# Queries' up-projection in six blocks of 512 columns a layer in place of eight of 384, and the later pairs' attention steps two or four slots later

## The chip, the cores and the metric

The kernel runs on one core of a Trainium2 chip. The metric is the device time of one execution in microseconds. TensorE is called PE in the profile (its weight loads PEld), VectorE DVE, ScalarE ACT, GpSimd POOL, SyncE SP.

## The reference, cut to what matters

Two layers of a streaming encoder at 256 positions, width 2048, all in float32. Each layer reads one input projection and has two branches. What the change touches is the attention branch and, through the order of work, the end of the convolution branch:

```
q  = (rmsnorm(q_down)  @ w_uq ).reshape(.., 16 heads, 192)   # 128 plain + 64 rotary columns a head
kv = (rmsnorm(kv_down) @ w_ukv).reshape(.., 16 heads, 256)   # 128 key + 128 value columns a head
q  = rmsnorm(q, q_norm_g); k = rmsnorm(k ++ k_pe, k_norm_g)  # over a head's 192 columns
q, k = rope on the last 64 columns
o  = chunk-causal softmax attention, then * silu(m_gate), @ w_proj_mla
u  = silu(layernorm(depthwise conv of width 31 (c_a * sigmoid(c_glu)))) * silu(c_gate)
y  = sigmoid(g_conv) * (u @ w_proj_conv) + sigmoid(g_mla) * (o @ w_proj_mla);  x + y @ w_out
```

## The kernel before, in words

**Pieces.** Every product has 256 positions (two halves t = 0, 1 of 128 as stationary operands) and streams weight columns in blocks of at most 512. A block comes in pieces of two 128-row slices of the weights: 8 pieces for a weight of 2048 rows, 2 for one of 512 rows (`wuq`, `wukv`). To keep float32's precision each weight piece is split into a rounded part `hi` (ScalarE: CAST hi<-raw) and the rest `lo` (VectorE: lo<-raw,hi), and so are the activations. A piece is 12 matmuls: 2 slices x 2 halves x 3 terms (high by hi, low by hi, high by lo). Layer 0 has 344 pieces. All instructions pass through a helper, so that every row of the profile says L126, and each engine does its work in the order in which the program issues it.

**How far the engines run ahead.** `product` (L337) issues for piece i first the load, `hi` of piece i + 3 (four `hi` buffers) and `lo` of piece i + 2 (three `lo` buffers), then the 12 matmuls, then `background`. So `lo` of piece i + 2 takes the buffer of piece i - 1.

**Slots.** `background` (L243) ends each piece: one piece is one slot. It runs the steps that `at_slot(n, f)` has put n slots ahead, and then, as far as a budget of VectorE time a slot lets it, the next entries of `fill`, a queue that holds the 31 taps of the convolution of every channel block, then the layernorm over channels (sum, mean by a matmul `mu`, centring, squares, variance by a matmul `var`, factors, `apply` and silu) and `gated`, the product with the turned gate. What `gated` leaves is split into `ycT` (`separated`: hi by ScalarE, lo by VectorE), in four groups c = 0 to 3 of four channel slices, that is of two pieces each.

**The queries' block.** Heads go in pairs b = 0 to 7. The order of a layer has for each pair `uq` (one block of 384 columns: both heads' 192), `ukv` (512 columns), then one long block of 8 pieces (`glu` or `cgate`). `uq_evac` (L685) copies the block out of PSUM on ScalarE and sums the squares; `rotate_q` turns the rotary part on VectorE; the rest of a pair's attention are steps at fixed slots behind `ukv` (STATS_AT 2 to O_AT 34). Products alternate between two pairs of PSUM banks, so a block's evacuation must be over before the next block but one begins.

**The place that forces work.** The convolution's projection (`pconv`, weights `wpc`) begins with piece 281 of layer 0. Ahead of the matmuls of its first block's piece j (p0 to p7 below) stands

```
def before_pconv(j, keep=keep):
    c = j * KS // 4
    while c not in keep["separated"]:
        run_fill()
    pay(keep["separated"][c])
    finish_late()
```

If group c has not been split by then, this issues what is missing at once: after `lo` of piece j + 2, which `product` has issued just before, and ahead of the matmuls of piece j.

Of the kernel before, what the change touches and what calls it, by code (L numbers as in the profile page):

```python
# [19 lines left out]
P = 128  # L20
T = 2
# [66 lines left out]
def order_of_layer():  # L88

    order = [("glu", 0, "win")] + [("down", i, "win") for i in range(len(DOWN_BLOCKS))]  # L90
    order += [("glu", 1, "win"), ("glu", 2, "win")]
    for b in range(NPAIR):
        order += [("uq", b, "wuq"), ("ukv", b, "wukv")]
        if b + 3 < 8:
            order.append(("glu", b + 3, "win"))
        elif b + 1 < NPAIR:
            order.append(("cgate", b - 5, "win"))
    for kind, s in (
        ("cgate", "win"), ("mgate", "win"), ("gmla", "win"), ("pmla", "wpm"),
        ("gconv", "win"), ("pconv", "wpc"), ("wout", "wo"),  # L100
    ):
        order += [(kind, i, s) for i in range(2 if kind == "cgate" else 0, 4)]
    return order


def blocks_of_layer():

    s = {"win": [], "wuq": [], "wukv": [], "wpc": [], "wpm": [], "wo": []}
    for kind, i, stream in order_of_layer():
        s[stream].append(DOWN_BLOCKS[i][1] if kind == "down" else 2 * QK if kind == "uq" else 512)  # L110
    return s


# [1 line left out]
def trunk(ctx: ExitStack, tc: tile.TileContext, xT, x, g_in, pos, win, wuq, wukv, wpc, wpm, wo, cst, rows, invf, out):  # L115
# [108 lines left out]
    def at_slot(ahead, f, vec=0.0, act=0.0, first=False):  # L224
        steps.insert(0 if first else len(steps), (clock[0] + ahead, (vec, act), f))
# [344 lines left out]
    for l in range(DEPTH):  # L570
# [86 lines left out]
        def attention_tiles(A=A, l=l):  # L657
            qk_t = big.tile([P, 16 * SEQ], F32R, tag="big", name=f"qk_t{l}")
            A.nope_t = qk_t[:, : 8 * SEQ].rearrange("p (i h s) -> p i h s", i=4, h=2)
            A.rope_t = qk_t[:, 8 * SEQ : 12 * SEQ].rearrange("p (i h s) -> p i h s", i=2, h=2)  # L660
            A.rope_k = qk_t[:, 10 * SEQ : 14 * SEQ].rearrange("p (i h s) -> p i h s", i=2, h=2)
            A.rope_l = qk_t[:, 12 * SEQ : 14 * SEQ].rearrange("p (h s) -> p h s", h=2)
            gps.memset(A.rope_l.bitcast(F32), 0.0)
            pv = big.tile([P, 4096], F32R, tag="big", name=f"pv{l}")
            A.pt = pv[:, : 2 * 768].rearrange("p (i h q) -> p i h q", i=2, h=2)
            v_parts = [pv[:, 1536 + i * 512 : 2048 + i * 512] for i in range(5)] + [qk_t[:, 14 * SEQ :]]
            v_parts = [a.rearrange("p (t h d) -> p t h d", t=T, h=2) for a in v_parts]
            A.v_split = [v_parts[2 * j : 2 * j + 2] for j in range(3)]
# [3 lines left out]
        def pair_of(b, A=A):
            if b not in A.pairs:


                A.pairs[b] = dict(
                    qk=work2.tile([P, T, 4, 6, 32], F32, tag="qk", name="qk"),
                    qr=work2.tile([P, T, 2, 2, HALF], F32, tag="qr", name="qr"),
                    vh=A.v_split[b % 3][0],
                    vl=A.v_split[b % 3][1],  # L680
                    ss=small.tile([P, 2, T, 2], F32, tag="ss_p", name="ss_p"),
                )
            return A.pairs[b]

        def uq_evac(b, t, ps, pair_of=pair_of):  # L685

            p = pair_of(b)
            act.copy(p["qk"][:, t, :, 0:2, :], ps[:, : 2 * NOPE].rearrange("p (j h c) -> p j h c", j=4, h=2))
            act.copy(p["qr"][:, t].rearrange("p a h c -> p (a h c)"), ps[:, 2 * NOPE :])
            for h in range(2):  # L690
                junk = work.tile([P, 512], F32, tag="junk", name="junk")
                act.activation(
                    junk[:, :QK].rearrange("p (j c) -> p j c", c=32),
                    ps.rearrange("p (j h c) -> p j h c", h=2, c=32)[:, :, h, :],
                    AF.Square, accum_out=p["ss"][:, 0, t, h : h + 1],
                )

        def rotate_q(b, pair_of=pair_of, ccq=ccq, ssq_t=ssq_t):
            p = pair_of(b)
            both = lambda a: a.rearrange("p t (a c) -> p (t a) c", a=2).unsqueeze(2).broadcast_to([P, 2 * T, 2, HALF])  # L700
            qa = work.tile([P, T, 2, 2, HALF], F32, tag="qa", name="qa")
            qb = work.tile([P, T, 2, 2, HALF], F32, tag="qb", name="qb")
            qr = p["qr"].rearrange("p t a h c -> p (t a) h c")
            vec.tensor_mul(qa.rearrange("p t a h c -> p (t a) h c"), qr, both(ccq))
            vec.tensor_mul(qb.rearrange("p t a h c -> p (t a) h c"), qr, both(ssq_t))
            out = p["qk"][:, :, :, 4, :].rearrange("p t (h a) c -> p t h a c", h=2)
            vec.tensor_sub(out[:, :, :, 0, :], qa[:, :, 0], qb[:, :, 1])
            vec.tensor_add(out[:, :, :, 1, :], qb[:, :, 0], qa[:, :, 1])

        def ukv_evac(b, t, ps, pair_of=pair_of):  # L710

            p = pair_of(b)
# [12 lines left out]
        def attention(b, pair_of=pair_of, ss_d=ss_d, kpe=kpe, ccq=ccq, ssq_t=ssq_t, gqk=gqk, A=A):  # L725
            p, st = pair_of(b), {}
            nope_t, rope_t, rope_k, rope_l = A.nope_t, A.rope_t, A.rope_k, A.rope_l
            qk, ss = p["qk"], p["ss"]

            def stats():  # L730

                st["r"] = small.tile([P, 2, T, 2], F32, tag="r_p", name="r_p")
                flat = lambda a: a.rearrange("p a t h -> p (a t h)")
                vec.tensor_add(flat(ss), flat(ss), flat(ss_base))
                rsqrt(flat(st["r"]), flat(ss), gps)
                st["rs"] = st["r"][:, 0]

            def scale_k():
# [20 lines left out]
            def back_in(name):  # L759
                for d, a in st[name]:  # L760
                    fetch(d, a)
# [115 lines left out]
                A.pairs.pop(b)  # L877

            at_slot(STATS_AT, stats, 0.6)
            at_slot(SCALE_AT, scale_k, 0.45, 1.1)  # L880
            at_slot(QK_BACK_AT, lambda: back_in("qk"), first=True)
            at_slot(QK_TURN_AT, blockwise, 1.85)
            at_slot(NOPE_AT, split_nope, 0.0, 1.8)
            at_slot(ROPE_AT, split_rope, 0.0, 2.5)
            at_slot(SCORES_AT, scores, 1.85, 0.35)
            at_slot(EXP_AT, exponentials, 0.0, 3.3)
            at_slot(P_BACK_AT, lambda: back_in("p"))
            at_slot(P_TURN_AT, turn_p, 0.9)
            at_slot(P_SPLIT_AT, split_p, 0.0, 0.8)
            at_slot(VALUES_AT, values)  # L890
            at_slot(O_AT, outputs, 0.62, 0.6)
# [353 lines left out]
        for kind, i, pl in planned:  # L1245
# [22 lines left out]
            elif kind == "uq":  # L1268
                if i == 0:
                    attention_tiles()  # L1270
                product(pl, of_down(0), lambda t, ps, i=i: uq_evac(i, t, ps), costs=(0.0, 2.3))
                at_slot(EVAC_AT + 1, lambda i=i: rotate_q(i), 1.2)
            elif kind == "ukv":
                product(pl, of_down(4), lambda t, ps, i=i: ukv_evac(i, t, ps), costs=(0.0, 2.6))
                attention(i)
                if i == NPAIR - 1:
                    layernorm()
            elif kind == "mgate":
# [64 lines left out]
def _layout(inp):  # L1343
# [7 lines left out]
    for l in range(DEPTH):  # L1351
# [9 lines left out]
    )  # L1361

    pair = lambda n, m: np.arange(2 * n).reshape(2, n)[:, :m].reshape(2, m // 32, 32).transpose(1, 0, 2).reshape(-1)
    val = np.concatenate([h * (NOPE + VH) + NOPE + np.arange(VH) for h in range(2)])
    cols_of = {
        "wuq": np.concatenate([2 * QK * b + pair(QK, QK) for b in range(NPAIR)]),
        "wukv": np.concatenate(
            [2 * (NOPE + VH) * b + np.concatenate([pair(NOPE + VH, NOPE), val]) for b in range(NPAIR)]
        ),
# [36 lines left out]
```

## Time and profile before

| | |
|---|---|
| Time, median of 3 runs | 1877.83 us (1877.79 to 1878.21) |
| The profiled execution | 1877.73 us, of which its span is 1875.9 us |
| PE busy | 1871.8 us (100% of the span) |
| DVE busy | 1577.1 us (84%) |
| ACT busy | 1366.4 us (73%) |
| POOL busy | 486.0 us (26%) |
| mean DMA rate | 237 GB/s |

The time is the span and 1.8 us around it. The span is cut into what each engine did; a row of a timeline gives the start, the time taken, the engine, the operation with the tiles it writes and reads, and how many like it follow. A matmul's row lasts from its issue to its modelled end, longer than the distance to the next matmul, so that the pace of PE is read from starts.

### The profile page before, as it was taken

The page shows a single profiled execution, that of the slowest core. Times are in us where ns is not written, and L with a number is a line of the kernel's source. Part 1 is how long each engine was busy: PE and PEld are TensorE (multiplying, and loading weights), DVE is VectorE, ACT ScalarE, POOL GpSimd, SP SyncE. Part 2 cuts the span into 40 slices and gives each one's busy share as a digit, 9 for nine tenths or more (in the row PEclk, how much of TensorE's full clock was granted, in tenths as well). Part 3 has the DMA queues.
Part 4 walks back from the last instruction along what each step waited for, and adds up shares of the span by engine and source line. Part 5 has one row for each costly group of instructions (what it writes and reads, how often), then busy time and mean ns, then how long its engine had stood idle before and what let it go on. Part 6 is the DMA issues. An engine that isn't in the chain of part 4 may idle for free.

```text
span 1875.9 us, 27403 instructions
## 1 busy us (share of the span) xinstructions
PE 1871.8 (100%) x8673; PEld 1584.2 (84%) x8673; DVE 1577.1 (84%) x2426; ACT 1366.4 (73%) x2468; POOL 486.0 (26%) x942
## 2 busy tenths in 40 slices
PE   9999999999999999999999999999999999999999
PEld 8988888888888888888899888888888888888887
DVE  6898988989999988766679889888899999885664
ACT  7678988888888766544557688888889878474442
POOL 1055555432200000122221555555322000001210
PEclk9999999999999999999999999999999999999999
DMA  9677878777765566678877787887777556667775
GB/s 330 216 258 262 272 242 273 264 241 233 244 204 193 195 208 214 212 237 283 288 231 217 250 272 257 262 279 242 245 237 248 191 196 203 206 209 218 242 249 167
DMA packets 140113, 445.06 MB, mean 237 GB/s; under 512 B 23808, under 2 KB 29440, under 8 KB 139968
## 3 DMA queue, kind: packets, MB, share of 16 engines
q1 hardware_dynamic: 106272, 359.89, 58.9%
q0 software_dynamic: 32832, 82.62, 13.5%
q8 instruction: 68, 1.11, 0.2%
q10 hardware_dynamic: 864, 0.80, 0.1%
q14 instruction: 77, 0.63, 0.1%
HBM read 399.18 MB, written 44.04 MB: 236 GB/s over the span
## 4 chain that ended last, share of the span: by engine, by line
PE 100%; DVE 0%; issue 0%
PE acc L126 97%; PE s L126 2%; PE o_ps L126 1%; PE warm L126 0%; PE acc_end L126 0%; PE var L126 0%; PE mu L126 0%; DVE xres L126 0%
## 5 line engine op out<-in xcount | busy, mean ns | idle before, releaser
L126 ACT CAST hi<-raw 128x1024 fp32r<-128x1024 f32 (+3 forms) x690 | 700.8, 1021 | 408.0 <-PE acc L126 347.4
L126 DVE TENSOR_TENSOR lo<-raw,hi 128x1024 fp32r<-128x1024 f32 (+3 forms) x690 | 814.5, 1182 | 197.2 <-PE acc L126 148.3
L126 PE MATMUL acc<-hi,hT 128*128 128x512 f32 (+2 forms) x1728 | 419.5, 382 | 0.0
L126 PEld LDWEIGHTS acc<-hi,hT 128*128 128x128 f32 x1728 | 319.7, 188 | 59.2
L126 PE MATMUL acc<-hi,h_hi 128*128 128x512 f32 (+2 forms) x864 | 260.9, 383 | 0.0
L126 PE MATMUL acc<-hi,h_lo 128*128 128x512 f32 (+2 forms) x864 | 260.3, 382 | 0.0
L126 ACT ACTIVATE tap<-u_t,cst 128x256 f32<-128x256 f32 x588 | 254.7, 499 | 3.2 <-DVE v_t L126 3.2
L126 PE MATMUL acc<-lo,h_hi 128*128 128x512 f32 (+2 forms) x864 | 229.7, 382 | 0.0
L126 PE MATMUL acc<-lo,hT 128*128 128x512 f32 (+2 forms) x864 | 229.3, 382 | 0.0
L126 DVE TENSOR_TENSOR v_t<-v_t,tap 128x512 f32<-128x512 f32 x294 | 201.9, 687 | 10.1
L126 POOL DMA_DIRECT2D turned<-turn_d x88 | 49.3, 560 | 539.8 <-DVE v_t L126 314.7
L126 PEld LDWEIGHTS acc<-hi,h_lo 128*128 128x128 f32 x864 | 161.3, 188 | 30.2
L126 PEld LDWEIGHTS acc<-lo,h_hi 128*128 128x128 f32 x864 | 160.6, 188 | 30.1
L126 PEld LDWEIGHTS acc<-lo,hT 128*128 128x128 f32 x864 | 160.6, 188 | 29.9
L126 PEld LDWEIGHTS acc<-hi,h_hi 128*128 128x128 f32 x864 | 160.3, 188 | 29.5 <-ACT hi L126 0.4
L126 POOL DMA_DIRECT2D turn_d<-gate x184 | 100.3, 553 | 325.4 <-DVE gate L126 182.6
L126 DVE SCALAR_TENSOR_TENSOR v_t<-u_t,cst,v_t 128x256 f32<-128x256 f32 x372 | 159.5, 479 | 2.3
L126 PE MATMUL acc<-hi,ycT 128*128 128x512 f32 x512 | 127.8, 389 | 0.0
L126 PE MATMUL acc<-hi,oT 128*128 128x512 f32 x512 | 127.8, 389 | 0.0
L126 PE MATMUL acc<-hi,yT 128*128 128x512 f32 x508 | 126.8, 389 | 0.0
L126 PE MATMUL acc<-hi,qkc 128*128 128x512 f32 (+1 forms) x512 | 118.7, 363 | 0.0
L126 PEld LDWEIGHTS acc<-hi,ycT 128*128 128x128 f32 x512 | 96.1, 188 | 20.0
(173 smaller groups left out, 2213.6 us busy)
## 6 DMA issues: line engine op xcount, KB each, us to landing
raw<-in_win SPq DMA_DIRECT2D x382, 512.0 KB, 4.3
raw<-in_wpm SPq DMA_DIRECT2D x64, 512.0 KB, 3.3
raw<-in_wpc SPq DMA_DIRECT2D x64, 512.0 KB, 4.1
raw<-in_wo SPq DMA_DIRECT2D x64, 512.0 KB, 4.7
raw<-in_wukv SPq DMA_DIRECT2D x32, 512.0 KB, 3.7
turned<-turn_d POOLq DMA_DIRECT2D x56, 256.0 KB, 4.8
raw<-in_win SPq DMA_DIRECT2D x32, 384.0 KB, 4.6
raw<-in_wuq SPq DMA_DIRECT2D x32, 384.0 KB, 3.4
```

The source lines that it names most:

```text
L126: ins = getattr(self.engine, name)(*a, **k)
```

## The change

Columns of the queries' weights are laid out anew: per four pairs b, b+1, b+2, b+3 three blocks of 512 hold [plain b, rotary b, rotary b+1], [plain b+1, rotary b+2, rotary b+3] and [plain b+2, plain b+3] (256 plain or 128 rotary columns each). Pairs 3 and 7 have no `uq` block of their own. So a layer has six `uq` blocks of two pieces (12 pieces of 512 columns) in place of eight (16 of 384), and 340 pieces and slots in place of 344.

The plain part of pairs 3 and 7 is parked in the last two heads of `o_sb` and copied on later (`waiting_in`); the rotary squares of pairs other than 0 and 4 are summed apart (`rope_squares`: one ScalarE and one VectorE instruction) and added in `stats`. From pair 3 on all attention steps but `stats` stand 2 slots later behind `ukv` (`d = 2`), for pair 7 4 slots later.

```
     for b in range(NPAIR):
-        order += [("uq", b, "wuq"), ("ukv", b, "wukv")]
+        order += [("uq", 3 * (b // 4) + b % 4, "wuq")] if b % 4 < 3 else []
+        order.append(("ukv", b, "wukv"))
...
+            A.waiting = A.o_sb[:, N_HEADS - 2 :, :].rearrange("p h s -> p (h s)").rearrange("p (t j h c) -> p t j h c", t=T, j=4, h=2)
...
+        def nope_out(b, t, src, A=A, part_of=part_of):
+            if b % 4 == 3:
+                act.copy(A.waiting[:, t].rearrange("p j h c -> p (j h c)"), src)
+            else:
+                act.copy(part_of(b, "qk")[:, t, :, 0:2, :], src.rearrange("p (j h c) -> p j h c", j=4, h=2))
...
+        def rope_squares(b, part_of=part_of):
+            sq = work.tile([P, T, 2, 2, HALF], F32, tag="qa", name="sq")
+            act.activation(sq, part_of(b, "qr"), AF.Square)
+            late.append(lambda: vec.tensor_reduce(part_of(b, "ss")[:, 2], sq.rearrange("p t a h c -> p t h a c"), axis=AX.XY, op=ALU.add))
+
+        def waiting_in(b, A=A, part_of=part_of, squares_of=squares_of):
+            act.copy(part_of(b, "qk")[:, :, :, 0:2, :].rearrange("p t j h c -> p (t j) h c"), A.waiting.rearrange("p t j h c -> p (t j) h c"))
+            for t in range(T):
+                squares_of(b, t, A.waiting[:, t])
+
+        def uq_evac(i, t, ps, nope_out=nope_out, rope_out=rope_out, squares_of=squares_of):
+
+            b = 4 * (i // 3)
+            cols = lambda a: a.rearrange("p (j h c) -> p j h c", h=2, c=32)
+            if i % 3 == 0:
+                nope_out(b, t, ps[:, :256])
+                rope_out(b, t, ps[:, 256:384])
+                rope_out(b + 1, t, ps[:, 384:])
+                squares_of(b, t, cols(ps[:, :384]))
+            elif i % 3 == 1:
+                nope_out(b + 1, t, ps[:, :256])
+                rope_out(b + 2, t, ps[:, 256:384])
+                rope_out(b + 3, t, ps[:, 384:])
+                squares_of(b + 1, t, cols(ps[:, :256]))
+            else:
+                nope_out(b + 2, t, ps[:, :256])
+                nope_out(b + 3, t, ps[:, 256:])
+                squares_of(b + 2, t, cols(ps[:, :256]))
...
+            d = 2 * ((b + 1) // 4)
...
-            at_slot(SCALE_AT, scale_k, 0.45, 1.1)
+            at_slot(SCALE_AT + d, scale_k, 0.45, 1.1)
...
+                d = 2 * (i // 4)
+                if i % 4 < 3:
+                    at_slot(3 + d, lambda i=i: rope_squares(i + 1), 0.4, 0.4)
+                if i % 4 < 2:
+                    at_slot(6 + d, lambda i=i: rotate_q(i + 1), 1.2)
+                elif i % 4 == 2:
+                    at_slot(6 + d, lambda i=i: waiting_in(i + 1), 0.0, 1.6)
+                    at_slot(7 + d, lambda i=i: rotate_q(i + 1), 1.2)
```

**Where it moves instructions, first: the projection of the convolution branch in layer 0.** The matmul of the mean stands behind piece 256 of 344 before and behind piece 255 of 340 now; the projection begins with piece 281 before and 277 now, so 25 pieces lay between them and 22 do now. VectorE's order there before, from `lo` of p2 (lo_8026) to that of p5 (lo_8093); ycT_7834 is the low part, the first `ycT` row is that of c = 2 (for p4 and p5), the second that of c = 3 (for p6 and p7):

```order
L126 TENSOR_TENSOR lo_8026<-raw_7908,hi_8003 128x1024
L126 TENSOR_TENSOR ycT_7834<-v_t,ycT_7833 128x512 x2
L126 TENSOR_TENSOR lo_8050<-raw_7935,hi_8028 128x1024
L126 STREAM_TRANSPOSE turned<-turned 128x512
L126 TENSOR_TENSOR v_t<-turned,v_t 128x2x128 x2
L126 TENSOR_TENSOR lo_8071<-raw_7959,hi_8052 128x1024
L126 TENSOR_TENSOR ycT_7834<-v_t,ycT_7833 128x512 x2
L126 TENSOR_TENSOR lo_8093<-raw_7980,hi_8073 128x1024
```

VectorE's order there now, from `lo` of p6 (lo_8027) over p7 (lo_8051) and the next block's p0 (lo_8072) to its p1 (lo_8097):

```order
L127 TENSOR_TENSOR lo_8027<-raw_7921,hi_8004 128x1024
L127 TENSOR_TENSOR v_t<-turned,v_t 128x2x128 x2
L127 TENSOR_TENSOR ycT_7860<-v_t,ycT_7859 128x512 x2
L127 TENSOR_TENSOR lo_8051<-raw_7947,hi_8029 128x1024
L127 STREAM_TRANSPOSE turned<-turned 128x512
L127 TENSOR_TENSOR v_t<-turned,v_t 128x2x128 x2
L127 TENSOR_TENSOR lo_8072<-raw_7967,hi_8053 128x1024
L127 STREAM_TRANSPOSE turned<-turned 128x512
L127 TENSOR_TENSOR v_t<-turned,v_t 128x2x128 x2
L127 TENSOR_TENSOR ycT_7860<-v_t,ycT_7859 128x512 x2
L127 TENSOR_TENSOR lo_8097<-raw_7985,hi_8074 128x1024
```

The `ycT` of c = 2 stood behind `lo` of p2 and stands behind `lo` of p6; that of c = 3 stood behind `lo` of p4 and stands behind `lo` of p8, the next block's first. In layer 1 the last `ycT` stands ahead of the projection's first `lo` in both kernels. ScalarE has now, from `hi` of p6, first a table load, four silus (v_t), `hi` of p7, the two `ycT` casts of c = 2, `hi` of p8 and p9, and the two casts of c = 3.

**Second: PE at p4 now.** Its order, with what each row waits for (ycT_7859 is the high part, ycT_7860 the low part, acc_0 and acc_1 the banks of the two halves):

```order
L127 MATMUL acc_1_7942<-lo_7963,ycT_7859 128x512 x2
L127 MATMUL acc_0_7941<-hi_7965,ycT_7859 128x512 [waits Activation_49]
L127 MATMUL acc_0_7941<-hi_7965,ycT_7859 128x512
L127 MATMUL acc_0_7941<-hi_7965,ycT_7860 128x512 [waits DVE_49]
L127 MATMUL acc_0_7941<-hi_7965,ycT_7860 128x512
L127 MATMUL acc_1_7942<-hi_7965,ycT_7859 128x512 x2
```

The order of the matmuls is that of before; the first row of p4 (hi_7965) waits for ScalarE's cast of c = 2 and the third for VectorE's low part, which now stand behind `lo` of p6 on their engine. p6 has the same two waits for c = 3.

**Third: ScalarE around the evacuation of the `uq` blocks issued with pairs 5 and 6.** Its order now with pair 5 (su is the evacuation of the `glu` block ahead of `uq`, pr the exponentials of an earlier pair, qk, qr and junk the evacuation of `uq`, first half):

```order
L127 CAST hi_3329<-raw_3188 128x1024
L127 ACT_TABLE_LOAD
L127 ACTIVATE su<-acc_0_3057,rinv_x 128x256
L127 ACTIVATE su<-acc_1_3058,rinv_x 128x256
L127 ACT_TABLE_LOAD
L127 ACTIVATE pr,rinv<-sx,nb,r_p 128x4x32 x2
L127 ACTIVATE pr,rinv<-s_3266,nb,r_p 128x2x4x32 x2
L127 CAST hi_3377<-raw_3216 128x1024
L127 CAST hi_3406<-raw_3251 128x1024
L127 COPY qk<-acc_0_3325 128x4x64
L127 COPY qr<-acc_0_3325 128x128 x2
L127 ACTIVATE junk,ss_p<-acc_0_3325 128x128 x2
```

Before, the exponentials with their table load stood two `hi` casts ahead of the `su` rows with theirs; now both stand in one slot, two `hi` casts ahead of the evacuation of `uq`.

## Rows read from the trace of the kernel before

**Rows 1.** The page: busy time, slices and the chain that ended last, by engine.

```profile
PE 1871.8 (100%) x8673; PEld 1584.2 (84%) x8673; DVE 1577.1 (84%) x2426; ACT 1366.4 (73%) x2468; POOL 486.0 (26%) x942
...
PEclk9999999999999999999999999999999999999999
...
PE 100%; DVE 0%; issue 0%
```

**Rows 2.** Who waited for whom: engine, line, releaser: us, times, longest.

```profile
ACT hi L126 <- PE acc L126: 347.4, 272, 2.6
...
DVE lo L126 <- PE acc L126: 148.3, 115, 2.3
```

**Rows 3.** PE's timeline, first pair: start us, us, instruction, count.

```profile
118.86 1.57 PE L126 MATMUL acc<-hi,qkc 128*128 128x384 f32 x8
...
123.05 2.01 PE L126 MATMUL acc<-hi,qkc 128*128 128x512 f32 x8
...
128.53 0.62 PE L126 MATMUL acc<-hi,h_hi 128*128 128x512 f32 x2
```

**Rows 4.** PE's timeline, convolution's projection, first block, layer 0.

```profile
765.21 1.98 PE L126 MATMUL acc<-hi,ycT 128*128 128x512 f32 x8
...
778.81 1.98 PE L126 MATMUL acc<-hi,ycT 128*128 128x512 f32 x8
```

**Rows 5.** Groups by form, VectorE: count | busy, mean ns of one | idle.

```profile
L126 DVE TENSOR_TENSOR v_t<-turned,v_t 128x256 f32<-128x256 f32 x32 | 11.7, 419 | 0.3
```

**Rows 6.** VectorE's timeline in that projection (idle before and releaser in brackets).

```profile
769.18 1.29 DVE L126 TENSOR_TENSOR ycT<-v_t,ycT 128x512 fp32r<-128x512 f32 x2 [1.49 <-ACT ycT L126]
770.39 1.22 DVE L126 TENSOR_TENSOR lo<-raw,hi 128x1024 fp32r<-128x1024 f32 x1
771.52 0.70 DVE L126 STREAM_TRANSPOSE turned<-turned 128x512 f32<-128x512 f32 x1
772.26 0.76 DVE L126 TENSOR_TENSOR v_t<-turned,v_t 128x256 f32<-128x256 f32 x2
...
774.08 1.28 DVE L126 TENSOR_TENSOR ycT<-v_t,ycT 128x512 fp32r<-128x512 f32 x2
...
779.07 1.23 DVE L126 TENSOR_TENSOR lo<-raw,hi 128x1024 fp32r<-128x1024 f32 x1 [1.44 <-PE acc L126]
```

**Rows 7.** ScalarE's timeline in that projection.

```profile
760.07 2.08 ACT L126 ACTIVATE v_t<-v_t,cst 128x256 f32<-128x256 f32 x4
...
766.08 1.28 ACT L126 ACT_TABLE_LOAD   x1
...
768.53 1.14 ACT L126 CAST ycT<-v_t 128x512 fp32r<-128x512 f32 x2
...
772.78 1.14 ACT L126 CAST ycT<-v_t 128x512 fp32r<-128x512 f32 x2 [1.21 <-DVE v_t L126]
...
778.11 1.05 ACT L126 CAST hi<-raw 128x1024 fp32r<-128x1024 f32 x1 [1.62 <-PE acc L126]
```

**Rows 8.** The page's groups: the weight load of that projection.

```profile
L126 PEld LDWEIGHTS acc<-hi,ycT 128*128 128x128 f32 x512 | 96.1, 188 | 20.0
```

**Rows 9.** ScalarE's timeline around one evacuation of the queries' product, layer 1.

```profile
1215.70 0.50 ACT L126 ACTIVATE pr<-sx,nb,r_p 128x128 f32<-128x128 f32 x1
...
1217.75 2.08 ACT L126 CAST hi<-raw 128x1024 fp32r<-128x1024 f32 x2
...
1221.15 0.84 ACT L126 ACTIVATE su<-acc,rinv_x 128x256 f32<-128x256 f32 x2
...
1225.16 0.36 ACT L126 COPY qk<-acc 128x256 f32<-128x256 f32 x1
...
1227.57 1.04 ACT L126 CAST hi<-raw 128x1024 fp32r<-128x1024 f32 x1
```

**Rows 10.** The chain in order of time: one pair's product with the values.

```profile
1219.20 1.16 PE o_ps L126 x8
```

**Rows 11.** PE's timeline from the start of the span.

```profile
0.78 4.39 PE L126 MATMUL warm<-const-float32-0.0 128*128 128x256 f32 x19 [0.78 <-PEq L1395]
```

More of the change, by code (lines that the diff above doesn't have):

```diff
@@ L109, in blocks_of_layer @@
     for kind, i, stream in order_of_layer():
-        s[stream].append(DOWN_BLOCKS[i][1] if kind == "down" else 2 * QK if kind == "uq" else 512)
+        s[stream].append(DOWN_BLOCKS[i][1] if kind == "down" else 512)
     return s
@@ L669, in attention_tiles @@
             A.o_sb = big.tile([P, N_HEADS, SEQ], F32, tag="big", name=f"o_sb{l}")
+            A.waiting = A.o_sb[:, N_HEADS - 2 :, :].rearrange("p h s -> p (h s)").rearrange("p (t j h c) -> p t j h c", t=T, j=4, h=2)
             A.rinv = layer_c.tile([P, T, N_HEADS], F32, tag="rinv", name="rinv")
[L672 to L689, printed above, removed]
+        def part_of(b, what, A=A):
+            p = A.pairs.setdefault(b, {})
+            if what not in p:
+                if what == "qk":
+                    p[what] = work2.tile([P, T, 4, 6, 32], F32, tag="qk", name="qk")
+                elif what == "qr":
+                    p[what] = work2.tile([P, T, 2, 2, HALF], F32, tag="qr", name="qr")
+                elif what == "ss":
+                    p[what] = small.tile([P, 3, T, 2], F32, tag="ss_p", name="ss_p")
+                else:
+                    p[what] = A.v_split[b % 3]["vl" == what]
+            return p[what]
@@ L690, in uq_evac, with rope_out, squares_of @@
+        def nope_out(b, t, src, A=A, part_of=part_of):
[3 more added lines that the diff above has]
+                act.copy(part_of(b, "qk")[:, t, :, 0:2, :], src.rearrange("p (j h c) -> p j h c", j=4, h=2))
+        def rope_out(b, t, src, part_of=part_of):
+            act.copy(part_of(b, "qr")[:, t].rearrange("p a h c -> p (a h c)"), src)
+        def squares_of(b, t, src, i=0, part_of=part_of):
             for h in range(2):
@@ L691, in uq_evac @@
                 junk = work.tile([P, 512], F32, tag="junk", name="junk")
+                j = src.shape[1]
                 act.activation(
-                    junk[:, :QK].rearrange("p (j c) -> p j c", c=32),
-                    ps.rearrange("p (j h c) -> p j h c", h=2, c=32)[:, :, h, :],
-                    AF.Square, accum_out=p["ss"][:, 0, t, h : h + 1],
-                )
-        def rotate_q(b, pair_of=pair_of, ccq=ccq, ssq_t=ssq_t):
-            p = pair_of(b)
+                    junk[:, : 32 * j].rearrange("p (j c) -> p j c", c=32), src[:, :, h, :],
+                    AF.Square, accum_out=part_of(b, "ss")[:, i, t, h : h + 1],
+                )
@@ new lines, in uq_evac @@
+        def uq_evac(i, t, ps, nope_out=nope_out, rope_out=rope_out, squares_of=squares_of):
[11 more added lines that the diff above has]
+                squares_of(b + 1, t, cols(ps[:, :256]))
+            else:
+                nope_out(b + 2, t, ps[:, :256])
+                nope_out(b + 3, t, ps[:, 256:])
+                squares_of(b + 2, t, cols(ps[:, :256]))
@@ L700, in rotate_q @@
+        def rotate_q(b, part_of=part_of, ccq=ccq, ssq_t=ssq_t):
+            p = {what: part_of(b, what) for what in ("qr", "qk")}
             both = lambda a: a.rearrange("p t (a c) -> p (t a) c", a=2).unsqueeze(2).broadcast_to([P, 2 * T, 2, HALF])
@@ L708, in rotate_q, with ukv_evac @@
             vec.tensor_add(out[:, :, :, 1, :], qb[:, :, 0], qa[:, :, 1])
-        def ukv_evac(b, t, ps, pair_of=pair_of):
-            p = pair_of(b)
+        def ukv_evac(b, t, ps, part_of=part_of):
+            p = {what: part_of(b, what) for what in ("qk", "vh", "vl", "ss")}
             k = ps[:, : 2 * NOPE].rearrange("p (j h c) -> p j h c", j=4, h=2)
@@ L723, in ukv_evac, with attention @@
                 )
-        def attention(b, pair_of=pair_of, ss_d=ss_d, kpe=kpe, ccq=ccq, ssq_t=ssq_t, gqk=gqk, A=A):
-            p, st = pair_of(b), {}
+        def attention(b, part_of=part_of, ss_d=ss_d, kpe=kpe, ccq=ccq, ssq_t=ssq_t, gqk=gqk, A=A):
+            p, st = {what: part_of(b, what) for what in ("qk", "vh", "vl", "ss")}, {}
+            d = 2 * ((b + 1) // 4)
             nope_t, rope_t, rope_k, rope_l = A.nope_t, A.rope_t, A.rope_k, A.rope_l
@@ L733, in stats @@
                 flat = lambda a: a.rearrange("p a t h -> p (a t h)")
-                vec.tensor_add(flat(ss), flat(ss), flat(ss_base))
-                rsqrt(flat(st["r"]), flat(ss), gps)
+                vec.tensor_add(flat(ss[:, :2]), flat(ss[:, :2]), flat(ss_base))
+                if b % 4:
+                    vec.tensor_add(ss[:, 0], ss[:, 0], ss[:, 2])
+                rsqrt(flat(st["r"]), flat(ss[:, :2]), gps)
                 st["rs"] = st["r"][:, 0]
@@ L879, in attention @@
             at_slot(STATS_AT, stats, 0.6)
-            at_slot(SCALE_AT, scale_k, 0.45, 1.1)
[L881 to L891, printed above, removed]
+            at_slot(SCALE_AT + d, scale_k, 0.45, 1.1)
+            at_slot(QK_BACK_AT + d, lambda: back_in("qk"), first=True)
+            at_slot(QK_TURN_AT + d, blockwise, 1.85)
+            at_slot(NOPE_AT + d, split_nope, 0.0, 1.8)
+            at_slot(ROPE_AT + d, split_rope, 0.0, 2.5)
+            at_slot(SCORES_AT + d, scores, 1.85, 0.35)
+            at_slot(EXP_AT + d, exponentials, 0.0, 3.3)
+            at_slot(P_BACK_AT + d, lambda: back_in("p"))
+            at_slot(P_TURN_AT + d, turn_p, 0.9)
+            at_slot(P_SPLIT_AT + d, split_p, 0.0, 0.8)
+            at_slot(VALUES_AT + d, values)
+            at_slot(O_AT + d, outputs, 0.62, 0.6)
         us, vs, keep = {}, {}, {"separated": {}}
@@ L1270, in trunk @@
                     attention_tiles()
-                product(pl, of_down(0), lambda t, ps, i=i: uq_evac(i, t, ps), costs=(0.0, 2.3))
-                at_slot(EVAC_AT + 1, lambda i=i: rotate_q(i), 1.2)
+                product(pl, of_down(0), lambda t, ps, i=i: uq_evac(i, t, ps), costs=(0.0, 2.5))
+                if i % 3 == 0:
+                    at_slot(EVAC_AT + 1, lambda i=i: rotate_q(4 * (i // 3)), 1.2)
             elif kind == "ukv":
@@ L1363, in _layout @@
     pair = lambda n, m: np.arange(2 * n).reshape(2, n)[:, :m].reshape(2, m // 32, 32).transpose(1, 0, 2).reshape(-1)
+    nope, rope = np.split(pair(QK, QK), [2 * NOPE])
+    queries = [(0, nope), (0, rope), (1, rope), (1, nope), (2, rope), (3, rope), (2, nope), (3, nope)]
     val = np.concatenate([h * (NOPE + VH) + NOPE + np.arange(VH) for h in range(2)])
     cols_of = {
-        "wuq": np.concatenate([2 * QK * b + pair(QK, QK) for b in range(NPAIR)]),
+        "wuq": np.concatenate([2 * QK * (4 * g + b) + part for g in range(2) for b, part in queries]),
         "wukv": np.concatenate(
```

## The prediction, on record before the changed kernel ran

> **What bounds the kernel now.** I read the page first: PE is busy for all of the span, the chain that ended last is PE and nothing else, and the granted clock stands at its full level in every slice [rows 1]. The list of waits comes next: ScalarE and VectorE wait for PE, 347.4 us ahead of `hi` casts and 148.3 us ahead of `lo` casts [rows 2], and the chain shows no time in which PE waited for them. So two things move the time: the pace of PE over the instructions it has, and any new wait of PE. Everything the other engines do more or less is hidden as long as `hi`, `lo`, the stationary tiles and free PSUM banks come in time. How far ahead they are, and where that is used up, is what the rest is about.
>
> **What the change removes.** The `uq` block of the first pair runs from 118.86 to 123.05, 4.19 us for 24 matmuls of 384 columns, 174.6 ns each; the `ukv` block behind it, 24 of 512 columns, from 123.05 to 128.53 [rows 3]. Five pieces of 12 matmuls of 512 columns take 778.81 - 765.21 = 13.60 us [rows 4], 2.72 us a piece, 226.7 ns a matmul and 5.44 us for 24. A column so costs less in the wider matmul: 53.3 ns would be 128 columns at 2.4 GHz, and 52.1 ns is the difference of the two paces, so that some 14 ns a matmul are fixed. Eight blocks of 4.19 are 33.52 us, six of 5.44 are 32.64; two layers give back 2 x 0.88 = 1.76 us. By the one `ukv` block (5.48) it would be 1.28. I take 1.7.
>
> The Trainium skill (TensorE: Matmul & The Clock Gate, "Wait — 56ns, not 53.3ns?") gives a fixed cost of about 2.5 ns a matmul at the full clock. By it 96 fewer matmuls would give back only 0.24 us, an estimate from that page; this case's rows disagree with it, about 14 ns a matmul [rows 3, 4], and the measurement decides.
>
> **What it adds elsewhere.** Twelve squares, twelve reductions and twelve small additions come in over both layers (six of each a layer), and four copies. No VectorE instruction of them has more elements than the 128x256 product of 419 ns [rows 5], so VectorE gets at most 24 x 0.42 = 10 us, against 1875.9 - 1577.1 = 299 us in which it is idle [rows 1]. ScalarE's squares and copies are at most of the size of a 128x512 cast, 0.6 us each, 10 us in all, against 510 us idle. I cost them at nothing; what hides them is the lead of `lo` (two pieces) and `hi` (three). Without that lead they would cost what they take. The weights' bytes are the same, in 24 loads of 512 KB in place of 32 of 384; the loads, the turns on POOL's queue and the fetches keep their distances in slots from the steps that use them, and POOL works a quarter of the span [rows 1]. Nothing is asked there.
>
> **What it makes late.** The fill of the convolution is metered per slot, and a layer has four slots fewer. In layer 0 the mean now falls three pieces nearer to the projection, and the split of c = 2 and c = 3 lands where `before_pconv` forces it. Before, the low part of c = 3 was issued at 774.08 [rows 6] and first needed by p6, one piece after 778.81 [rows 4]: 7 us early. Now it stands on VectorE behind a `lo` that can only begin when PE has ended the piece just before the one that needs it. Nothing hides that: PE stands until it is done, and behind PE's waiting row stand all its others.
>
> The first wait, in us from the moment at which p4 would start without it (all steps from rows of the same stretch):
> - `lo` of p6 starts 0.26 later (779.07 against the piece's start at 778.81, and PE ended this idle time) [rows 4, 6].
> - The next VectorE instruction starts 1.13 after a `lo` (770.39 to 771.52) [rows 6]: 1.39. The first of the two `gated` products takes 0.42 [rows 5]: 1.81.
> - ScalarE's cast starts 0.10 after that (product at 772.26 for 0.42, cast at 772.78) [rows 6, 7]: 1.91.
> - ScalarE itself must be free: `hi` of p6 starts 0.70 ahead of a boundary (778.11 against 778.81) [rows 4, 7], a piece earlier; with the cast (1.05), the table load (1.28), four silus (2.08) and `hi` of p7 (1.05) [rows 7] that is -0.70 - 2.72 + 5.46 = 2.04. So the `ycT` cast starts at about 2.0.
> - The first of two casts is done 0.6 later (1.14 for two; the low part starts 0.65 after the cast, 768.53 to 769.18) [rows 6, 7]: 2.6. `ycT` is the stationary operand, so a weight load of 0.19 [rows 8] and a hand-over of some 0.05 follow: PE starts at 2.85.
> - PE has two matmuls (0.45), then needs the low part: 2.0 + 0.65 + 0.65 [rows 6] + 0.24 = 3.55, where PE is at 3.30: another 0.25.
>
> Together **3.1 us**. The second, at p6, has a turn of the gate ahead of the product, 0.74 (771.52 to 772.26) [rows 6], and no silus: 0.26 + 1.13 + 0.74 + 0.42 + 0.10 = 2.65, + 0.6 + 0.24 = 3.49, + 0.25 = **3.7 us**. p5 and p7 use the second cast of each group, ready 0.6 later, in time. What is late next is nothing: `lo` of the following pieces again waits for PE. In layer 1 no such row is forced.
>
> The operation no row shows is PE's restart after such a wait, four times. Bounds: without a visible weight load (4 x 0.19 less, waits of 6.0) and with twice it (4 x 0.19 more, 7.6). I take the middle, 6.8, since the load's row is the nearest.
>
> Sum, against the profiled execution's own time: 1877.73 - 1.7 + 6.8 = 1882.8; the median of the runs is 0.10 above that execution, so **1882.9 us**, 0.27% slower. With the bounds of both terms, 1882.1 to 1884.1.
>
> **The rivals.**
>
> *The waits are covered.* If the forced steps ran while PE was still in p3 and p5, only the pace would be left: 1877.8 - 1.7 = 1876.1. One of two covered gives about 1879.5. For it speaks that VectorE has 16% idle time; against it that `lo` casts end their idle time on PE [rows 2, 6], so that VectorE can't get ahead. It decides from waits of 5.5 us downward (3.8 for 0.2%, which is about what a measurement of this kernel can tell from no change, and 1.7 to offset the pace). Chance 0.17.
>
> *ScalarE holds a PSUM bank.* With pairs 5 and 6 two table loads, an evacuation and the exponentials now stand in one slot ahead of the evacuation of `uq`. From the start of `uq`: `hi` ends at 0.35, table load 1.28, `su` 0.84, table load 1.28, exponentials 2.05 (1215.70 to 1217.75), `hi` twice 2.08: 7.9. The evacuation took 2.4 (1225.16 to 1227.57) [rows 9] and has up to two copies of 0.36 more: 11.0. PE needs the bank after `uq`, the values' 1.16 [rows 10] and `ukv`: 5.44 + 1.16 + 5.44 = 12.04. About 1 us is left, half with pair 6, whose `gate` evacuation is longer. It decides from 1 us unseen: then each 0.5 us costs 2 us over the four places, about 1885. Chance 0.07.
>
> *The clock falls.* PE stands still for nearly 3 us twice. No row before has PE idle at the full clock, and the granted clock never falls [rows 1]. The warm-up's 19 matmuls of 256 columns took 4.39 us [rows 11], 231 ns each, where the two paces above give 122 ns for 256 columns: that is the lower level, 1.2 GHz. If the wait at p6 brought it back for as long, half of 4.39 us would be lost: 1885.1. The Trainium skill (TensorE: Matmul & The Clock Gate, "HAM oscillation — how this bites in real kernels") says that idle gaps of PE between bursts of matmuls can return it to half rate; no run here shows it yet. Chance 0.06.
>
> **How the numbers follow.** The forecast has 0.70, the rivals 0.17, 0.07 and 0.06. Of the forecast's 0.70 I count 0.04 as within 0.2%; of the first rival 0.02 as faster by over 0.2%, for work that leaves the path somewhere I don't see. So faster 0.02, same 0.19, slower 0.79. The range reaches from 1880.0, within the first rival, to 1886.0, past the two others; some 0.13 is left below and 0.03 above.
>
> **What would show it.** Right: PE's `uq` blocks at 5.44 us each, six a layer; in the list of waits, PE behind ScalarE's and VectorE's `ycT`, two of about 2.8 and 3.5 us and two of 0.25, in layer 0 alone; VectorE's `lo` behind PE as before. Wrong: PE's chain without a row for `ycT` of either engine; waits of PE at a `glu` or `cgate` block behind ScalarE; a granted clock below full; a pace of 512 columns other than 226.7 ns.

## The result, and the profile after

The changed kernel takes 1884.96 us (median of 6 executions, 1884.47 to 1885.70), the kernel before beside it on the same chip 1877.78 (6, 1877.31 to 1878.21): ratio 1.0039, 95% interval 1.0026 to 1.0051. It is slower, by 7.2 us where 5.1 were predicted, and inside the range. Its profiled execution took 1884.47 us, that of before 1877.73.

The page of the changed kernel, instructions of PE and the chain by engine, beside [rows 1]:

```profile
PE 1872.1 (99%) x8577; PEld 1571.8 (83%) x8577; DVE 1582.8 (84%) x2452; ACT 1361.7 (72%) x2456; POOL 493.0 (26%) x942
...
PE   9999999999999999899999999999999999999999
...
PEclk9999999999999999999999999999999999999999
...
PE 99%; DMA 1%; DVE 0%; ACT 0%; issue 0%; SPq 0%; ACTq 0%
```

PE has 96 matmuls fewer, and one slice in which it is not quite busy. Which wait that is stands in the list of waits of PE alone (us in total, times, longest):

```profile
PE acc L127 <- ACT ycT L127: 5.6, 2, 3.2
PE acc L127 <- ACT hi L127: 1.0, 1, 1.0
PE warm L127 <- PEq L1445: 0.8, 1, 0.8
```

Two waits for `ycT`, none for a PSUM bank; the 1.0 us behind `hi` belongs to the first loads and comes up at the end of this section. The place of the two is in PE's timeline of the convolution's projection, first block, layer 0 (p3, then p4, p5, p6 and the first row of p7):

```profile
773.14 1.98 PE L127 MATMUL acc<-hi,ycT 128*128 128x512 f32 x8
...
778.43 2.39 PE L127 MATMUL acc<-hi,ycT 128*128 128x512 f32 x8 [2.41 <-ACT ycT L127]
...
781.56 1.98 PE L127 MATMUL acc<-hi,ycT 128*128 128x512 f32 x8
...
787.60 3.54 PE L127 MATMUL acc<-hi,ycT 128*128 128x512 f32 x8 [3.16 <-ACT ycT L127]
790.98 1.07 PE L127 MATMUL acc<-lo,ycT 128*128 128x512 f32 x4
791.88 1.52 PE L127 MATMUL acc<-hi,ycT 128*128 128x512 f32 x6
```

A piece takes 2.72 us [rows 4]. So p4 was due at 773.14 + 2.72 = 775.86 and starts 2.57 later; it lasts 3.13, 0.41 more than a piece. p6 was due at 784.28 and starts 3.32 later; it lasts 4.28, 1.56 more. VectorE's timeline shows what PE waits for (`lo` of p6, then `gated` and the low part of c = 2; from 784.53 on `lo` of p8, the turn, `gated`, the low part of c = 3):

```profile
776.11 1.23 DVE L127 TENSOR_TENSOR lo<-raw,hi 128x1024 fp32r<-128x1024 f32 x1
777.26 0.76 DVE L127 TENSOR_TENSOR v_t<-turned,v_t 128x256 f32<-128x256 f32 x2
778.41 1.29 DVE L127 TENSOR_TENSOR ycT<-v_t,ycT 128x512 fp32r<-128x512 f32 x2 [0.39 <-ACT ycT L127]
...
784.53 1.22 DVE L127 TENSOR_TENSOR lo<-raw,hi 128x1024 fp32r<-128x1024 f32 x1
785.68 0.70 DVE L127 STREAM_TRANSPOSE turned<-turned 128x512 f32<-128x512 f32 x1
786.41 0.76 DVE L127 TENSOR_TENSOR v_t<-turned,v_t 128x256 f32<-128x256 f32 x2
787.58 1.29 DVE L127 TENSOR_TENSOR ycT<-v_t,ycT 128x512 fp32r<-128x512 f32 x2 [0.40 <-ACT ycT L127]
```

`lo` begins 0.25 after the moment at which the waiting piece was due, and what stands behind it follows without a gap, but for the 0.4 us in which VectorE itself waits for ScalarE's cast of the high part (the first row for c = 2, the second for c = 3):

```profile
777.76 1.13 ACT L127 CAST ycT<-v_t 128x512 fp32r<-128x512 f32 x2
...
786.93 1.14 ACT L127 CAST ycT<-v_t 128x512 fp32r<-128x512 f32 x2 [2.26 <-DVE v_t L127]
```

The 1.56 us are something else. The stretches of 4 us (length, busy time of PE, PEld, DVE, ACT, POOL, the granted clock, DMA share, GB/s):

```profile
780.00:784.00 4.00, 4.00 (x19) 3.33 (x18) 2.21 (x4) 1.44 (x2) 0.00 (x0) 1.00 0.03 11
784.00:788.00 4.00, 0.84 (x3) 0.42 (x3) 3.43 (x7) 1.74 (x3) 0.00 (x0) 0.92 0.67 209
788.00:792.00 4.00, 4.00 (x13) 3.11 (x13) 0.87 (x2) 0.89 (x2) 0.00 (x0) 0.66 0.13 53
792.00:796.00 4.00, 4.00 (x20) 3.30 (x19) 2.37 (x2) 1.29 (x2) 0.00 (x0) 1.00 0.37 130
```

Around the end of the second wait the granted clock falls for about 3 us and comes back; the page's slices of 47 us show a 9 over all of it. The `uq` block of the first pair runs from 119.56 to 125.00, 5.44 us as predicted, and the `ukv` block behind it from there to 130.44, 5.44 too, where it took 5.48 behind a block of 384 columns [rows 3]:

```profile
119.56 1.98 PE L127 MATMUL acc<-hi,qkc 128*128 128x512 f32 x8
...
125.00 1.98 PE L127 MATMUL acc<-hi,qkc 128*128 128x512 f32 x8
...
130.44 0.62 PE L127 MATMUL acc<-hi,h_hi 128*128 128x512 f32 x2
```

Over both layers, each block taken from its first start to the start behind it, sixteen `uq` blocks of 4.16 to 4.19 us became twelve of 5.44, 1.48 us less, and the sixteen `ukv` blocks went from 5.48 to 5.44 or 5.47, 0.45 less: 1.93 us in all.

Last, PE's third piece starts at 12.19 in this execution, at 11.46 in that of before, behind `hi` of the first loads of `in_win` (the 1.0 us of the list). The instructions are the same up to there; in the profiles of the kernels below it starts between 10.82 and 12.30, and no edit touches it. Sum for the profiled execution: -1.93 + (2.57 + 0.41) + (3.32 + 1.56) + 0.73 = 6.66 us, against 1884.47 - 1877.73 = 6.74.

### The profile page after: what moved, and what is told of

Read it like the earlier page. It is cut to its first block, busy times and chain, and to the rows that moved or that the text cites. A ratio compares the mean times of both kernels' runs of the same rounds, so it can differ in the third digit from the quotient of the medians.

```text
span 1882.7 us, 27123 instructions
## 1 busy us (share of the span) xinstructions
PE 1872.1 (99%) x8577; PEld 1571.8 (83%) x8577; DVE 1582.8 (84%) x2452; ACT 1361.7 (72%) x2456; POOL 493.0 (26%) x942
## 4 chain that ended last, share of the span: by engine, by line
PE 99%; DMA 1%; DVE 0%; ACT 0%; issue 0%; SPq 0%; ACTq 0%
PE acc L127 96%; PE s L127 2%; PE o_ps L127 1%; DMA raw<-in_win 0%; DMA gx<-in_g 0%; DVE lo L127 0%; ACT hi L127 0%; ACT v_t L127 0%; PE acc_end L127 0%; DVE turned L127 0%; ACT ycT L127 0%; DVE v_t L127 0%; PE mu L127 0%; PE var L127 0%; DVE xres L127 0%
## 5 line engine op out<-in xcount | busy, mean ns | idle before, releaser
L127 ACT ACTIVATE tap<-u_t,cst 128x256 f32<-128x256 f32 x568 | 246.5, 499 | 2.8 <-DVE v_t L127 2.8
L127 DVE TENSOR_TENSOR v_t<-v_t,tap 128x512 f32<-128x512 f32 x284 | 195.3, 688 | 9.5 <-DVE v_t L127 0.5
L127 DVE SCALAR_TENSOR_TENSOR v_t<-u_t,cst,v_t 128x256 f32<-128x256 f32 x392 | 167.8, 479 | 2.4
L127 PE MATMUL acc<-hi,qkc 128*128 128x512 f32 x448 | 115.4, 389 | 0.0
```

The source lines that it names most:

```text
L127: ins = getattr(self.engine, name)(*a, **k)
```

## The experiments

The theory: the loss is two forced splits that stand too late, and a clock that falls with the second wait. Rivals: the new blocks themselves cost something (their evacuations and squares), or VectorE is short of time there, so that earlier work is no help. All diffs are against the changed kernel, but for the first. Executions of the kernel before beside them had medians of 1877.66 to 1877.79.

**The two late splits without the new blocks.** The kernel before, whose fill stands still for five slots:

```
-        while fill and budget["vec"] > 0:
+        while fill and budget["vec"] > 0 and not 280 <= clock[0] < 285:
```

> The kernel before, blocks of 384 and eight uq blocks as they were; only the fill stands still for five slots from the 280th on, so that the splits of c = 2 and c = 3 are forced behind the low weights of p6 and p8, as in the changed kernel. Its turn of the gate for c = 3 lies one piece earlier than there, so that the second wait is 0.74 us shorter. Theory (the loss of the changed kernel comes from where the split is forced and from nothing in the new blocks): waits of PE for ycT of about 2.6 and 2.6 us and 0.4 us each for the low part, 1877.8 + 6.0 = 1883.8 us, and 1.3 us more if the clock falls after the second wait as it did in the changed kernel. Rival (the new evacuations or the new squares are part of the loss): less than 4 us over before.

1885.64 us (5 executions), 1.0042 of the kernel before, 1.0029 to 1.0054, near the 1885.1 that was worked out with the clock's fall. PE's p4, p6 and p7, and the stretch behind p6's start:

```profile
777.96 2.38 PE L126 MATMUL acc<-hi,ycT 128*128 128x512 f32 x8 [2.36 <-ACT ycT L126]
...
786.33 3.53 PE L126 MATMUL acc<-hi,ycT 128*128 128x512 f32 x8 [2.36 <-ACT ycT L126]
...
791.03 1.55 PE L126 MATMUL acc<-hi,ycT 128*128 128x512 f32 x6
```

```profile
788.00:792.00 4.00, 4.00 (x14) 3.17 (x13) 0.77 (x1) 1.05 (x1) 0.00 (x0) 0.67 0.01 5
```

Both waits are 2.52 us (p3 starts at 772.72 and p5 at 781.09, so that p4 and p6 were due at 775.44 and 783.81), and p6 lasts 4.70. The kernel with eight blocks of 384 loses as much as the changed one, and behind the first loads no other wait of PE is in the changed kernel's list: the first rival falls.

**The split asked for earlier.** One edit, three sizes; n = 1, 2 and 3:

```
-            c = j * KS // 4
+            c = min((j + n) * KS // 4, 3)
```

> As the kernel that asks two pieces earlier, but one piece earlier only: the split of c = 2 stands behind the low weights of p5 and that of c = 3 behind those of p7, one piece of 2.72 us ahead of where the changed kernel has them. Theory (the wait is the distance of the forced split from the matmul that needs it, and a piece earlier takes 2.72 us off): the first wait, 2.57 us, is covered and perhaps 0.3 us of low part left; of the second, 3.32 us, about 0.6 us is left; the clock stays full, since PE hardly stands; 1878 us, between 1877 and 1879. Rival (VectorE cannot get ahead of PE, a step asked for earlier runs as late as before): waits as in the changed kernel, about 1884.

> The changed kernel, with the forced split of a group asked for two pieces earlier: its VectorE part then stands behind the low weights of p4 (c = 2) and p6 (c = 3) in place of p6 and p8, and VectorE has two more pieces, 5.4 us, for work of about 3 us. Theory (the time over before is nothing but the two forced waits and what follows from them): PE's two waits for ycT, 2.57 and 3.32 us, are gone, p4 and p6 take 2.72 us like their neighbours, the granted clock is full in every stretch, and the time is 1884.96 - 7.9 = 1877.1 us, with the start's first pieces between 1876.2 and 1877.3: 0.03 to 0.09% under before. Rival (the waits come from VectorE having too much to do in this stretch, so that asking earlier only moves them to the hi and lo of the next pieces): new waits of 1 us or more on lo or hi in the same stretch, and a time of 1879 us or more.

> The changed kernel, with the forced split of a group asked for three pieces earlier: behind the low weights of p3 (c = 2) and p5 (c = 3). Two pieces earlier left 0.44 and 0.95 us ahead of p4 and p6 and 0.41 us of low part in each, 2.2 us in all, since VectorE's forced stretch is then longer: two turns and two pairs of products stand in it, its cast came 4.96 us after the start of the low weights' subtraction. Theory (with one more piece of 2.72 us both are covered, by about 2.3 us ahead of p4 and 0.5 us ahead of p6): no wait for ycT, or at most 0.3 us of low part at p6, and what is left is the pace alone: 1877.8 - 1.7 = 1876.1 us, 1875.7 to 1876.6. Rival (the forced stretch then holds up the low weights of the next pieces): a wait of 0.5 us or more for lo at p4 or p5, and 1877 us or more.

One piece earlier: 1880.35 us (1.0016, 1.0007 to 1.0025), with waits of 1.62 and 2.02. Two: 1878.10 (1.0001, 0.9993 to 1.0010), with 0.45 and 0.95. Three: 1876.25 (0.9991, 0.9982 to 0.9999), with none. Both guesses for one and two pieces were too low (with one piece the clock still fell in 4 of 11 executions), and the rival isn't right either: a piece earlier takes 0.95 to 1.3 us off a wait, not 2.72. VectorE with two pieces, c = 3 (the start is that of `lo` of p5 and p6):

```profile
777.62 2.35 DVE L127 TENSOR_TENSOR lo<-raw,hi 128x1024 fp32r<-128x1024 f32 x2
779.88 0.70 DVE L127 STREAM_TRANSPOSE turned<-turned 128x512 f32<-128x512 f32 x1
780.62 0.76 DVE L127 TENSOR_TENSOR v_t<-turned,v_t 128x256 f32<-128x256 f32 x2
781.30 0.70 DVE L127 STREAM_TRANSPOSE turned<-turned 128x512 f32<-128x512 f32 x1
782.04 0.76 DVE L127 TENSOR_TENSOR v_t<-turned,v_t 128x256 f32<-128x256 f32 x2
783.21 1.29 DVE L127 TENSOR_TENSOR ycT<-v_t,ycT 128x512 fp32r<-128x512 f32 x2 [0.41 <-ACT ycT L127]
```

Asked for later, the first turn and its products (1.4 us) have been done by the fill; asked for earlier, they stand in the forced stretch, too. For c = 2 two products of `apply` (1.29 us) and the four silus on ScalarE join them.

**The meter instead of the force.** The place that forces work is left as it is, and the fill gets 0.01 or 0.02 us more a slot:

```
-        slot = 12 * (n / 2400 + 0.0133) - 0.04
+        slot = 12 * (n / 2400 + 0.0133) - 0.03
```

> The changed kernel with one constant of the fill's budget other: 0.03 in place of 0.04 us held back in each slot, so that the fill gets 0.01 us more VectorE time a slot. The place that forces work is untouched. The splits of c = 2 and c = 3 then stand behind the low weights of p2 and p5, of their own accord and not by force (p6 and p8 in the changed kernel, p2 and p4 in the kernel before). Theory (four slots fewer, by which the fill is metered, are what made the splits late; 0.01 us in each of some 277 slots, 2.8 us of VectorE, is enough to make up for it): no wait for ycT, full clock, 1876.1 us, as when the split is asked for three pieces earlier. Rival (VectorE is short of time in this stretch, and the fill that comes earlier takes it from the low weights): PE waits for lo somewhere ahead of the projection, and the time is 1877 us or more.

> As the kernel with 0.03, but 0.02 us held back a slot: the splits of c = 2 and c = 3 stand behind the low weights of p1 and p3, a piece or two earlier still. Theory: nothing more to win, 1876.1 us again, with the splits 2.7 to 5.4 us earlier in the timeline. Rival: more fill a slot begins to eat the lead of the low weights in the attention's slots, with waits of PE for lo and 1877 us or more.

1875.78 us with 0.03 (0.9990, 0.9981 to 0.9999) and 1875.86 with 0.02 (0.9990, 0.9981 to 0.9999), 11 executions each. With 0.03 the only wait of PE left in the list, and the low parts of c = 2 and c = 3, needed by p4 at 774.96 and p6 at 780.40:

```profile
PE warm L127 <- PEq L1445: 0.8, 1, 0.8
```

```profile
768.04 1.30 DVE L127 TENSOR_TENSOR ycT<-v_t,ycT 128x512 fp32r<-128x512 f32 x2 [1.47 <-ACT ycT L127]
...
775.34 1.29 DVE L127 TENSOR_TENSOR ycT<-v_t,ycT 128x512 fp32r<-128x512 f32 x2
```

VectorE had the time; the meter held it back. With this the second rival falls, and the kernel beats both of the study, if by 0.1% only.

That the four slots fewer made the splits late is not shown by this, since 0.01 us more a slot would make up for another cause as well. The program's own count says otherwise. By the code a slot of n columns leaves the fill 12 x (n / 2400 + 0.0133) - 0.04 - (2n / 960 + 0.06) us of VectorE time: 1.18 for 384 columns, 1.55 for 512. Sixteen of the one are 18.9 us and twelve of the other 18.6, so that the four slots cost 0.24 us a layer. The six new squares are charged 0.4 us each (`at_slot(3 + d, ..., 0.4, 0.4)`), 2.4 us. In the program with that charge at 0, and nothing else changed, the mean stands behind piece 253, not 255, and the splits stand behind `lo` of p2 and p5 unforced, as with 0.03. In the kernel before with the charge added the mean stands behind piece 258, not 256, and the splits are not forced either. So of the three pieces by which the mean came nearer, two are the charge and one the slots. These are orders of instructions; neither program was run.

**The clock.** PE is kept at work in the waits, with products of zeros that nothing reads: in both, in the first alone (j == 4), in the second alone (j == 6):

```
             finish_late()
+            if l == 0 and j in (4, 6):
+                idle = tp_p.tile([P, 256], F32, tag="tp", name="idle")
+                n = 14 if j == 4 else 22
+                for i in range(n):
+                    pe.matmul(idle, zero.broadcast_to([P, P]), zero.broadcast_to([P, 256]), start=i == 0, stop=i == n - 1)
```

> The changed kernel, with 14 and 22 matmuls of 256 columns of zeros put ahead of p4 and p6 in the first block, into a bank of their own that nothing reads: PE is at work for about 1.7 and 2.7 us of the two waits, which are as long as before. Theory (the second wait costs more than its length because PE stands still and the granted clock then falls to 0.66 for about 4 us): the clock is full in every stretch, p6 takes about 3.0 us in place of 4.28, and the time is 1.3 to 2 us below the changed kernel, about 1883.2. Rival (p6 takes 4.28 us because the low part of its stationary tiles comes late, whatever the clock): p6 stays at 4.2 or more and the time at about 1885.

> The changed kernel with PE kept at work in the first wait alone (14 matmuls of zeros ahead of p4); the wait ahead of p6 is an idle one of 3.3 us. Filled both, the clock stayed full (1882.7 us); with none filled it fell to 0.66 behind the second wait (1885.0). Theory A (the second wait alone brings the clock down, being the longer): about 1884.5, p6 over 4 us, clock below full in 788 to 792. Theory B (it takes both waits, close behind each other: a wait of 2.57 us alone didn't, and 2.0 us as the second of two did in some executions): 1882.7 us, p6 3.13 us, full clock.

> The changed kernel with PE kept at work in the second wait alone (22 matmuls of zeros ahead of p6); the wait ahead of p4 is an idle one of 2.57 us. By both theories of the clock the first wait doesn't bring it down: 1882.7 us, full clock, p6 3.13 us. If the first wait's idling makes the clock fall later, at p6, whatever PE does by then: p6 over 4 us and about 1884.5.

And one wait left without any filling, by c = 2 asked for at p2 and c = 3 at p6, `c = (0, 0, 2, 2, 2, 2, 3, 3)[j]`:

> The changed kernel, with c = 2 asked for two pieces earlier (behind the low weights of p4, which left 0.44 and 0.41 us) and c = 3 as late as in the changed kernel (behind those of p8), so that only the second wait is there, without any filling. Theory of the sum: 1877.8 - 1.7 + 0.85 + 3.7 = 1880.7 us if the clock stays full (theory B of the clock, both waits are needed), 1882 to 1882.7 if it falls (theory A, the second alone is enough).

Both filled: 1882.73 us (1882.47 to 1883.07), 2.2 below the changed kernel, a little more than expected, though p4 and p6 start as late (p6 due at 783.83):

```profile
783.83 2.62 PE L127 MATMUL idle<-const-float32-0.0 128*128 128x256 f32 x22
787.15 2.39 PE L127 MATMUL acc<-hi,ycT 128*128 128x512 f32 x8 [0.70 <-ACT ycT L127]
789.37 1.07 PE L127 MATMUL acc<-lo,ycT 128*128 128x512 f32 x4
790.28 1.52 PE L127 MATMUL acc<-hi,ycT 128*128 128x512 f32 x6
```

```profile
788.00:792.00 4.00, 4.00 (x18) 3.31 (x19) 1.65 (x2) 1.06 (x1) 0.00 (x0) 1.00 0.04 11
```

p6 lasts 3.13, as p4 does: 0.41 goes to PE's restart and the low part, and the rest of the 1.56, 1.15, was the clock. First alone filled: 1885.15, nothing won; p6 lasts 5.28 (786.60 to 791.88) and the clock stands at 0.50, the lower level of 1.2 GHz, for a whole stretch:

```profile
784.00:788.00 4.00, 1.40 (x3) 1.12 (x4) 3.44 (x6) 1.14 (x2) 0.00 (x0) 0.75 0.55 198
788.00:792.00 4.00, 4.00 (x11) 3.08 (x10) 0.00 (x0) 1.04 (x1) 0.00 (x0) 0.50 0.00 0
792.00:796.00 4.00, 4.00 (x18) 3.25 (x17) 1.91 (x2) 1.06 (x1) 0.00 (x0) 0.90 0.37 127
```

Second alone filled: 1883.43, from 1881.96 to 1884.51. In the profiled execution the clock fell behind the first wait, which both theories had ruled out; p4 (777.53 to 781.91) lasts 4.38:

```profile
777.53 3.61 PE L127 MATMUL acc<-hi,ycT 128*128 128x512 f32 x8 [2.41 <-ACT ycT L127]
...
781.91 2.00 PE L127 MATMUL acc<-hi,ycT 128*128 128x512 f32 x8
```

```profile
776.00:780.00 4.00, 2.46 (x6) 1.95 (x7) 2.41 (x5) 2.00 (x4) 0.00 (x0) 0.67 0.54 190
780.00:784.00 4.00, 4.00 (x18) 3.20 (x17) 1.85 (x3) 1.06 (x2) 0.00 (x0) 0.90 0.00 0
```

The second alone, not filled: 1880.86 (1.0015, 1.0006 to 1.0024); its wait was 2.07 and not 3.3 us, since the fill, relieved of c = 2, had the last product of c = 3 done ahead of `lo` of p8 (0.63 more followed for the low part, which still stood behind it). So the median, though it is near theory B's 1880.7, decides nothing. The executions tell more; the mean granted clock is listed with each, the idle times are those of the one that was profiled:

| kernel | idle of PE ahead of p4, p6 (us) | executions below a mean clock of 1.000 |
|---|---|---|
| changed | 2.57, 3.32 | 6 of 6 |
| before, fill held back | 2.52, 2.52 | 5 of 5 |
| first wait filled | 0.85, 3.32 | 5 of 5 |
| second wait filled | 2.57, 0.70 | 5 of 9 |
| second wait alone | 0.45, 2.07 (and 0.63) | 7 of 11 |
| asked one piece earlier | 1.62, 2.02 | 4 of 11 |
| both filled; asked two pieces earlier | at most 0.95 | 0 of 19 |

Theory B falls (one wait is enough). Theory A holds for the wait of 3.32 us, but not in what it says of the first: one of 2.57 us alone brought the clock down in 5 of 9. At 2 to 2.6 us of idling the clock falls in some executions of the same program and not in others. The falls differ in length, too: a mean clock of 0.999 goes with about 3 us at the lower level (the profile of the changed kernel), 0.998 with about twice that (the profile with the first wait filled); of the changed kernel's six executions four have 0.998.

## Why the prediction was right, and where it was off

- **The pace**, -1.7: `uq` blocks of 5.44 us, and -1.93 by all blocks, 0.45 of it in the `ukv` blocks, which the prediction left as they were. With no wait left the kernels are 1.5 (asked three pieces earlier) and 1.9 us (0.03 a slot) under the kernel before. The fixed cost of the Trainium skill (TensorE: Matmul & The Clock Gate, "Wait — 56ns, not 53.3ns?") would have given 0.24, an estimate from that page; the rows and both medians give more.
- **Other engines' work at nothing**: right for their time; the changed kernel has no wait for `hi`, `lo` or a bank behind the first loads. But the 2.4 us a layer that the new squares are charged in the fill's meter are, by the program's count, most of what made the splits late. The prediction saw that they are late and where, and named the four slots fewer as the cause, which are one piece of three.
- **The two waits**, 6.8: with PE kept at work, where the clock plays no part, 2.57 + 0.41 + 3.32 + 0.41 = 6.71. The casts came 1.90 and 2.65 after the due times, worked out 2.0 and 2.65. PE's row begins 0.67 behind them, not 0.84, because it begins together with the weight load and not behind it; the load, the operation no row of before showed, then costs 0.11 inside the row (the second matmul starts 0.34 behind the first, at a pace of 0.23). The wait for the low part is 0.16 and has a restart of 0.11 behind it. Together they are 0.38 of the 0.41, where 0.25 stood. That part stands in no row of the list of waits, where the prediction looked for it, but in the length of PE's row, 2.39 in place of 1.98. The kernel with both waits filled took 1882.73 us, where 1882.9 stood.
- **Where it was off**: the rival "The clock falls" got a chance of 0.06, and it is what happened, in every execution, on top of the two waits; a granted clock below full was also one of the prediction's own signs of being wrong. That 1884.96 still lies in the range is due to the room left above for that rival. Its price was right for the median, 2.2 us: 1885.1 against 1884.96 measured, and with both waits filled 1884.96 - 1882.73 = 2.2 comes back. That is in part luck, since the length of the fall was taken from the warm-up, and a fall of the profiled execution's length costs 1.15. What failed is the step that the forecast took full speed for granted because no row of before showed a fall: no row of before had PE idle either [rows 1], so that the rows spoke for neither side. The rule named there, in the Trainium skill (TensorE: Matmul & The Clock Gate, "HAM oscillation — how this bites in real kernels"), is borne out by these runs: the clock at 0.92 and 0.66 around the end of the second wait, 1.00 with both filled.
- **The covered waits**, 0.17: didn't come true; its 1876.1 us is what the kernel takes when the split is asked for three pieces earlier, 1876.25.
- **ScalarE holds a PSUM bank**, 0.07: no such wait. The evacuation of `uq` with pairs 5 and 6 ends 1.18 and 0.87 us ahead of the need in layer 0; 1 us and half of that had been worked out.

## What to carry to other kernels

Work that is metered moves when the meter is charged with something new or has other slots to run in: 2.4 us of charges and four slots fewer made the fill three pieces late, and the place that forces it turned that into two stalls, each worth more than the whole gain. Look for such a meter before changing a block size or adding a step, even one that its engine has time for; 0.01 us a slot mended it here. And a stall of PE that was full until then can cost more than its length: here the clock fell in part of the executions with a wait of 2.0 to 2.6 us, and in all of those with two of 2.5 or one of 3.3, so allow for it when a kernel that never idled gets such a wait.

## What the runs showed of the hardware

The granted clock fell with idle stretches of PE of up to 2.0 us in 4 of 11 executions and in each of the 11 that had one of 3.3, and in none of the 19 whose longest was 0.95; it cost 1.15 us in the changed kernel's profiled execution (p6's 4.28 less 3.13) and 2.2 in the medians. Products of zeros in the waits kept it up in all 8 executions. One of the 70 executions of the kernel before that ran beside the experiments shows the same, 1881.39 us at a mean clock of 0.999; it was not profiled, so that its cause is open. Why executions of the same program with the same wait differ was not found out.
